# Two of the output product's four column blocks in the seven-product form, with the sums of its weights made earlier and kept in DRAM

## The chip, the core and the metric

The kernel runs on one core of a Trainium2 chip. TensorE (PE in the profile) multiplies matrices, with a weight-load side (PEld) that overlaps it; VectorE (DVE), ScalarE (ACT) and GpSimd (POOL) work element by element; SyncE (SP) issues transfers. Each engine runs its instructions in the order of its own list and waits on semaphores for the others. Transfers are issued from SP, ACT or POOL queues and carried by 16 DMA engines. SBUF is the core's working memory of 128 partitions, PSUM holds TensorE's results in eight banks of 128 x 512 fp32.

The metric is the device time of one execution in microseconds, as the median of the runs. The profile is of one execution, with times counted from the start of its span.

## The reference, cut to what matters

A decoder layer on 256 rows of 2048 channels, all in float32. The input projection gives the pieces for 16 heads of causal attention and for a short gated convolution, and the gates that merge the two:

```
h = _rmsnorm(x, pre_norm_g)
proj = jnp.einsum('bsd,de->bse', h, w_in)
...
y_mla = jnp.einsum('bse,ed->bsd', attn, w_o_mla)
...
y_conv = jnp.einsum('bse,ed->bsd', b_gate * conv * jax.nn.silu(z_conv), w_o_conv)
merged = jax.nn.sigmoid(g_mla) * y_mla + jax.nn.sigmoid(g_conv) * y_conv
out = jnp.einsum('bsd,de->bse', merged, w_out)
x = x + _rmsnorm(out, post_norm_g)
```

The change is in the last product, `merged` (256 x 2048) by `w_out` (2048 x 2048).

## The kernel before, in words

**Three matmuls for one product.** Every fp32 operand is split into a high part, rounded to the matmul's format, and a low part, the rest. A product is high x high + low x high + high x low. Weights come from DRAM in units of 128 x 2048 (1 MB); one unit holds four blocks of 128 contraction rows by 512 output columns. `load_raw` (L152) brings a unit into one of three buffers (tag raw) on SP's queue. `split_unit` (L176) splits it in two halves of 128 x 1024: ScalarE writes the high half (`whi`, L265), VectorE subtracts it from the raw weights (`wlo`, L266). There are five buffers each for high and low halves, two and a half units. `ahead` (L212) keeps loads three units and splits one unit ahead of `take` (L223), which hands a unit to the product.

**The stages.** First the latent products of the input, to about 50 us. Then 16 heads (L994 to L1113): each multiplies four units of channel weights (`channels`), and between them stand the gates' units (z), the keys', queries' and values' products, the scores, the softmax and the values of the head before. `next(form_steps)` is called three times in each of the heads 0 to 13; it runs a generator, `make_forms` (L869), one step at a time, which makes parts of sums of the normalised input on VectorE and ScalarE and stores them to DRAM from ScalarE's queue. The attention output of head group v lies in `at_f`, the channels' in `cv_f`; the blocks of groups 2 and 3 of both are first written in heads 8 and later.

From about 590 us the branch products (w_o_mla, w_o_conv, tag sq) are interleaved with the gate products g_mla and g_conv (tags sX, sY, sZ). Those gate products already use a seven-product form (Strassen's, in Winograd's arrangement): two column blocks by two halves of the contraction would take eight half products; seven products Q1, V5, V6, V7, V3, V4, Q2 of sums of input blocks (the forms) by sums of weight blocks give the same, with some additions on the results. Each is two units of 12 matmuls. Their PSUM banks are X (tag st), Z (tag cv) and Y (tag o).

Last comes the output product. The merged activations, turned so that the contraction lies on partitions, are written to DRAM in four blocks `far_m` and come back on the POOL queue into `turned_m` tiles; `split_turned` (L970) splits them into `m_b[0..3]`, for each of two row halves t one ScalarE and one VectorE instruction of 128 x 512. Blocks 2 and 3 are the last to be merged, at the end of the branch stage. Column block c needs units (c, 0..3), one for each `m_b[k]`; each plain unit is 24 matmuls (`out_products`, L1471): two row halves by four by three. The order is that of `out_order` (L145): (0,0), (0,1), (1,0), (1,1), (0,2), (1,2), (0,3), (1,3), then blocks 2 and 3. `out_block` (L1497) takes a finished PSUM bank: ScalarE squares it with a row sum, VectorE multiplies it by the gain into `og`. Block 3 runs row half by row half; `finish` and `finish_by_two` (L1527, L1533) then compute the row norm, add the residual `xr` (a 2 MB load on SP's queue, L1561) and store.

**What sets the order.** The program is traced in Python and a scheduler places each engine's instructions. An instruction that is wrapped in `keep_in_program_order` is placed behind the one traced just before it on its engine, whatever that was; one that is not wrapped may be moved ahead, as its data and the scheduler's estimate allow. All matmuls are kept. The splits of the output product's weights and of `m_b[2]` are not kept in the kernel before (`split_act`, L264, has `keep` False there); that of `m_b[3]` isn't either.

Of the kernel before, what the change touches and what calls it, by code (L numbers as in the profile page):

```python
# [82 lines left out]
def tile_layer(ctx: ExitStack, tc: tile.TileContext, xw, w0, xb, x, pos, pvec, post_g, wc, wz, wcv, wkr, wqk, wqr, wv, cwr, wsq, out):  # L83
# [92 lines left out]
    def split_unit(i):  # L176
# [22 lines left out]
        for h in range(0, w, HALF):  # L199
            n = min(HALF, w - h)  # L200
            if u_out[3, 0] <= i < u_out[3, 3]:
# [21 lines left out]
    def take(i):  # L223
        ahead(i)
        return pieces(splits.pop(i))
# [643 lines left out]
    def make_forms():  # L869
# [49 lines left out]
        while True:  # L919
            yield  # L920

    form, sums = {}, {}

# [6 lines left out]

    form_steps = make_forms()
    tap, coming, ps_by_head = None, [], {}
# [12 lines left out]

    def turned_unit(far, both, first, tag=None, queue=nc.sync):

# [3 lines left out]
        def load():  # L951
            name = f"turned_{both.name}{first}"
            if tag:
# [13 lines left out]

        return [[load if i == 0 else None, split(i), None, None] for i in range(len(far))]

# [24 lines left out]
    for h in range(H):  # L994
# [48 lines left out]
        if h < H - 2:  # L1043
            next(form_steps)
        if v and at == 0 or h == H - 1:
            next(tap)
# [21 lines left out]
        if h < H - 2:  # L1068
            next(form_steps)
        channels(h, 2)  # L1070
        if h < H - 2:
            next(form_steps)
        if h == H - 1:
            split_branch(1)
            bring_form("11")
# [48 lines left out]
    spool = right.enter_context(tc.tile_pool(name="spool", bufs=1, side="right", reuse_waits="tile"))  # L1124
    LAST = ("f5", "f6", "rb0", "rc0", "rc1", "rb1")
    last_parts = []
# [247 lines left out]
    m_b = Late("m", lambda i: spool.tile([P, 4, 2 * S], F32R, name=f"m_both{i}", tag=M_TAGS[i], bufs=1))  # L1374
    m_load = [turned_unit(far_m[a:b], m_b, a, tag, nc.gpsimd) for a, b, tag in ((0, 2, "rc0"), (2, 3, "rc1"), (3, 4, "rb1"))]

# [89 lines left out]
    assert not wanted and not fetched  # L1466

    m_load[1][0][0]()
    last_m = m_load[2][0]
# [9 lines left out]

    pss = [[bank(f"out{c}_{t}") for t in range(NT)] for c in range(2)]  # L1480
    for i, (c, kk) in enumerate(out_order[:4]):
        w = take(u_out[c, kk])
        if i == 0:
            last_m[0]()
        elif i == 2:
            m_load[1][0][1]()
        out_products(pss[c], w, kk)
    main.close()
# [7 lines left out]

    def out_block(c, t, ps):  # L1497
        cs = slice(512 * c, 512 * c + 512)
        junk = op.tile([P, 512], F32, name=f"junk{c}_{t}", tag="junk", bufs=2)
        nc.scalar.activation(junk[:, :], ps[:, :], AF.Square, accum_out=ssq[:, t, c : c + 1])  # L1500
        if c == 3 and t:
            return ps
        og_now = nc.vector.tensor_tensor(og[:, t, cs], ps[:, :], gb[:, cs], op=ALU.mult)
        if c == 3:
# [50 lines left out]

    for i, (c, kk) in enumerate(out_order[4:6]):
        w = take(u_out[c, kk])
        if i == 0:
            last_m[1]()
        out_products(pss[c], w, kk)  # L1560
    tc.keep_in_program_order(nc.sync.dma_start(out=xr[:, :, :], in_=x))  # L1561
    for c in range(3):
        if c == 2:
            pss.append([bank(f"out{c}_{t}") for t in range(NT)])
        for kk in range(4) if c == 2 else (3,):
            out_products(pss[c], take(u_out[c, kk]), kk)
        for t in range(NT):
            out_block(c, t, pss[c][t])
    nc.vector.reduce_sum(part[:, :], ssq[:, :, :3], axis=mybir.AxisListType.X)
    nc.vector.tensor_scalar(part[:, :], part[:, :], 1.0 / D, EPS, op0=ALU.mult, op1=ALU.add)  # L1570
    pss = [bank(f"out3_{t}") for t in range(NT)]
# [97 lines left out]
```

## Time and profile before

| | us |
|---|---|
| median of 3 runs (lowest, highest) | 1013.35 (1012.68, 1013.49) |
| the profiled execution's own time | 1013.55 |
| its span | 1011.8 |
| TensorE busy | 1004.2 (99%) |
| weight loads busy | 835.4 (83%) |
| VectorE busy | 811.4 (80%) |
| ScalarE busy | 586.3 (58%) |
| GpSimd busy | 170.7 (17%) |
| output product in the chain: start, length | 916.51, 87.05 |
| HBM read and written | 234.80 MB, 22.02 MB |

The granted TensorE clock is 1.00 in all the long stretches. A row of the chain of waits or of the timeline has the start, the length, the engine, what it writes and reads, and how many instructions are merged in it; in brackets stands the idle time before it and what ended that. A row of the busy time by stretch has the stretch, then for PE, PEld, DVE, ACT and POOL the busy time and the number of instructions, then the mean granted clock, the DMA engines' busy share and GB/s.

### The profile page before, as it was taken

The numbers are of one execution on the slowest core, as the hardware profiler recorded it, in microseconds if no ns is written. First come the engines' busy times: TensorE is split into PE (matmuls) and PEld (weight loads), VectorE is DVE, ScalarE is ACT, GpSimd is POOL, SyncE is SP. The second block draws the span as 40 slices with busy tenths as digits, with TensorE's granted clock in tenths as the row PEclk, the third lists the DMA queues.
The fourth block names the chain that finished last, engine by engine and source line by source line (L and its number), as shares of the span: only waits on it lengthen the run. The fifth ranks groups of instructions, "written<-read, shape, count | busy, mean of one in ns | idle before, by whom it ended". The sixth has DMA issues, their size and how long they took to land.

```text
span 1011.8 us, 12983 instructions
## 1 busy us (share of the span) xinstructions
PE 1004.2 (99%) x4552; PEld 835.4 (83%) x4552; DVE 811.4 (80%) x1111; ACT 586.3 (58%) x838; POOL 170.7 (17%) x311
## 2 busy tenths in 40 slices
PE   9999999999999999999999999999999999999997
PEld 7888888888888888888888888888888888888886
DVE  7588878868888689877797889898989779997562
ACT  7675656556556456555565465565675664674541
POOL 4620411113211223212133110000000001003000
PEclk9999999999999999999999999999999999999999
DMA  8785768568786668866689779897599989639742
GB/s 338 282 291 183 260 201 304 197 214 276 234 303 232 228 229 283 272 219 232 216 264 338 292 306 291 344 375 218 187 333 296 305 321 260 239 127 322 289 166 84
DMA packets 54369, 261.84 MB, mean 259 GB/s; under 512 B 8768, under 2 KB 13504, under 8 KB 29216
## 3 DMA queue, kind: packets, MB, share of 16 engines
q1 hardware_dynamic: 37728, 214.35, 57.7%
q0 software_dynamic: 12256, 38.13, 14.0%
q10 hardware_dynamic: 4320, 8.54, 2.4%
q8 instruction: 35, 0.57, 0.2%
q14 instruction: 30, 0.25, 0.1%
HBM read 234.80 MB, written 22.02 MB: 254 GB/s over the span
## 4 chain that ended last, share of the span: by engine, by line
PE 98%; DMA 1%; DVE 0%; ACT 0%; SPq 0%; issue 0%
PE cv L88 34%; PE sq L88 17%; PE sX L88 9%; PE z L88 9%; PE out L88 9%; PE sZ L88 4%; PE kn L88 2%; PE qn L88 2%; PE vv L88 2%; PE sY L88 2%; PE ckv L88 2%; PE qa L88 2%; PE qr L88 1%; PE o L88 1%; PE sw L88 1%; DMA raw<-xb_dram 1%
## 5 line engine op out<-in xcount | busy, mean ns | idle before, releaser
L265 ACT ACTIVATE whi<-raw 128x1024 fp32r<-128x1024 f32 (+1 forms) x302 | 306.1, 1028 | 236.7 <-PE cv L88 103.9
L266 DVE TENSOR_TENSOR wlo<-raw,whi 128x1024 fp32r<-128x1024 f32 (+1 forms) x300 | 352.7, 1188 | 101.2 <-ACT whi L265 74.6
L88 PE MATMUL cv<-whi,x_both 128*128 128x512 f32 x1024 | 319.8, 389 | 0.0
L88 PEld LDWEIGHTS cv<-whi,x_both 128*128 128x128 f32 x1024 | 192.3, 188 | 39.5
L88 PE MATMUL cv<-wlo,x_both 128*128 128x512 f32 x512 | 199.5, 390 | 0.0
L88 PEld LDWEIGHTS cv<-wlo,x_both 128*128 128x128 f32 x512 | 96.2, 188 | 19.4
L266 DVE TENSOR_TENSOR slo_V<-b,shi_V 128x1024 fp32r<-128x1024 f32 x60 | 71.5, 1218 | 15.9 <-PE sq L88 8.5
L265 ACT ACTIVATE shi_V<-b 128x1024 fp32r<-128x1024 f32 x60 | 61.5, 1053 | 39.2 <-PE sq L88 21.2
L88 PE MATMUL z<-whi,x_both 128*128 128x512 f32 x256 | 80.0, 389 | 0.0
L366 POOL DMA_DIRECT2D far<-via x64 | 35.4, 559 | 227.2 <-DVE via L358 217.2
L88 PE MATMUL sq<-whi,at_both 128*128 128x512 f32 x256 | 60.6, 389 | 0.0
L88 PE MATMUL sq<-whi,cv_both 128*128 128x512 f32 x256 | 60.6, 389 | 0.0
L88 PEld LDWEIGHTS sq<-whi,cv_both 128*128 128x128 f32 x256 | 48.0, 188 | 10.0
L88 PEld LDWEIGHTS sq<-whi,at_both 128*128 128x128 f32 x256 | 48.0, 188 | 10.0
L88 PEld LDWEIGHTS z<-whi,x_both 128*128 128x128 f32 x256 | 48.1, 188 | 9.9
L88 PE MATMUL z<-wlo,x_both 128*128 128x512 f32 x128 | 49.8, 389 | 0.0
L88 PE MATMUL out<-whi,m_both 128*128 128x512 f32 x208 | 49.4, 389 | 0.0
L88 PE MATMUL sX<-shi_V,form 128*128 128x512 f32 x192 | 47.4, 389 | 0.0
L88 PEld LDWEIGHTS out<-whi,m_both 128*128 128x128 f32 x208 | 39.0, 188 | 8.1
L88 PEld LDWEIGHTS sX<-shi_V,form 128*128 128x128 f32 x192 | 36.0, 188 | 7.5
L265 ACT ACTIVATE shi_Q<-b 128x1024 fp32r<-128x1024 f32 x28 | 28.8, 1052 | 21.5 <-PE sq L88 19.1
L1263 POOL DMA_DIRECT2D b<-wsq_dram x8 | 7.0, 869 | 193.4 <-DVE b L1272 76.8
(304 smaller groups left out, 1568.7 us busy)
## 6 DMA issues: line engine op xcount, KB each, us to landing
raw<-wcv_dram SPq DMA_DIRECT2D x64, 1024.0 KB, 6.2
raw<-wsq_dram SPq DMA_DIRECT2D x48, 1024.0 KB, 7.2
b<-wsq_dram SPq DMA_DIRECT2D x26, 1024.0 KB, 5.7
raw<-wz_dram SPq DMA_DIRECT2D x16, 1024.0 KB, 4.9
raw<-wqk_dram SPq DMA_DIRECT2D x8, 1024.0 KB, 6.8
b<-wsq_dram POOLq DMA_DIRECT2D x8, 1024.0 KB, 11.0
far_form<-form ACTq DMA_DIRECT2D x28, 256.0 KB, 3.3
form<-far_form SPq DMA_DIRECT2D x7, 1024.0 KB, 13.8
```

What stands on the lines that cost most here:

```text
L88: return tc.keep_in_program_order(nc.tensor.matmul(*a, **kw))
L265: a = nc.scalar.activation(hi, src, AF.Copy)
L266: b = nc.vector.tensor_tensor(lo, src, hi.bitcast(F32), op=ALU.subtract)
L366: tc.keep_in_program_order(queue.dma_start(out=f[i], in_=m))
L1263: tc.keep_in_program_order(nc.gpsimd.dma_start(out=dst[:, :], in_=wsq[n, c + b, k], accum_op=ALU.add))
```

## The change

Column blocks 1 and 2 of the output product are computed together by the seven products; blocks 0 and 3 stay plain, and block 3's units 0 and 1 are moved up into the middle, for both row halves. The input forms are made from the unsplit `turned_m` tiles: V7's from blocks 0 and 1 (A11 - A21) after the third plain unit; V5's, V6's and V3's from all four blocks in two parts, `m_forms(0)` ahead of plain unit (0,2) and `m_forms(1)` ahead of V5. Each part is three VectorE sums and three splits of 128 x 512.

The weight sums of V5, V7, V6 and V4 do not depend on the input, and are made in heads 1 to 7: a second generator, `make_sums`, stepped beside `make_forms`, loads four 512 KB pieces into the still unused parts of `at_f` and `cv_f` on SP's queue, adds them in four VectorE instructions of 128 x 1024 and stores four results to DRAM on ScalarE's queue, four times over. Later they are loaded as units like any other weights. There are now 22 units where there were 16. The products' matmuls are 8 x 24 + 14 x 12 = 360 where there were 384.

The splits of all output units, of `m_b[2]` and of `m_b[3]` are now kept in program order, and so are the copies of the PSUM banks that the seven products need in between (`copied`). The additions to them (`added`) and `out_block`'s instructions are not.

```diff
-    out_order = [(0, 0), (0, 1), (1, 0), (1, 1), (0, 2), (1, 2), (0, 3), (1, 3)]
-    out_order += [(c, k) for c in (2, 3) for k in range(4)]
-    u_out = {ck: add(wsq[4, ck[0], ck[1]]) for ck in out_order}
+    SUMS = ("V5", "V6", "V7", "V4")
+    far_sum = {(n, u): dram.tile([P, UNIT], F32, name=f"far_sum{n}_{u}") for n in SUMS for u in range(2)}
+    set_raw = {"Q1": (1, 0), "V3": (2, 2), "Q2": (1, 2)}
+    out_order = [(0, 0), (0, 1), (3, 0), ("Q1", 0), ("Q1", 1), (0, 2), (0, 3), ("V5", 0), ("V5", 1), ("V6", 0), ("V6", 1), (3, 1)]
+    out_order += [(n, u) for n in ("V7", "V3", "V4", "Q2") for u in range(2)] + [(3, 2), (3, 3)]
...
-            split_act(hi[:, :n], lo[:, :n], t[:, h : h + n], i in (u_head[0][1], *u_first, *u_d[0][2][:2]), i in (u_grp["r", 0], u_grp["v", 0], u_head[0][0]))
+            split_act(hi[:, :n], lo[:, :n], t[:, h : h + n], i in (u_head[0][1], *u_first, *u_d[0][2][:2]) or i >= u_out[0, 0], i in (u_grp["r", 0], u_grp["v", 0], u_head[0][0]))
...
+    def make_sums():
...
+        for _ in range(3):
+            yield
+        for i in range(4):
+            if i:
+                put(i - 1, (2, 3))
+            bring(i, (0, 1))
+            yield
+            bring(i, (2, 3))
+            yield
+            yield
+            plus(a, a, b)
+            plus(b, b, c)
+            yield
+            put(i, (0, 1))
+            plus(c, a, c)
+            plus(d, c, d)
+            yield
+        put(3, (2, 3))
...
+    def m_part(n, j, src, sign=1.0):
+        ks = slice(4 * j, 4 * j + 4)
+        hi, lo = (m_form[n][:, ks, i, :] for i in range(2))
+        keep = tc.keep_in_program_order
+        keep(nc.scalar.activation(hi, src, AF.Copy, scale=sign))
+        if sign == 1.0:
+            keep(nc.vector.tensor_tensor(lo, src, hi.bitcast(F32), op=ALU.subtract))
...
+    def m_forms(j):
+        u = m_sum(0, j, m_raw(2 + j, 1), m_raw(j, 1), ALU.subtract)
+        w = m_sum(1, j, quarters(u), m_raw(j, 0), ALU.add)
+        m_part("V5", j, u)
+        m_part("V6", j, w, -1.0)
+        w = m_sum(1, j, quarters(w), m_raw(2 + j, 0), ALU.subtract)
+        m_part("V3", j, w)
...
+    for i, (c, kk) in enumerate(out_order[:3]):
+        if i == 0:
+            last_m[0]()
+        plain_products(c, kk)
+    m_form_7()
     main.close()
...
+    def copied(name, b, tag):
+        res[name] = wide(f"o{name}", tag)
+        tc.keep_in_program_order(nc.scalar.activation(res[name][:, :], set_bank[b][:, :], AF.Copy))
+
+    def added(name, b):
+        nc.vector.tensor_tensor(res[name][:, :], res[name][:, :], set_bank[b][:, :], op=ALU.add)
+
+    set_products("Q1", 0)
+    set_products("Q1", 1)
+    copied("a", "X", "d")
+    m_load[1][0][1](True)
+    m_forms(0)
+    plain_products(0, 2)
+    last_m[1](True)
+    plain_products(0, 3)
+    m_forms(1)
+    set_products("V5", 0)
+    for t in range(NT):
+        out_block(0, t, pss[0][t])
+    set_products("V5", 1)
     tc.keep_in_program_order(nc.sync.dma_start(out=xr[:, :, :], in_=x))
...
+    set_products("V6", 0)
+    copied("c", "Z", "a")
+    set_products("V6", 1)
+    copied("b", "X", "b")
+    plain_products(3, 1)
+    for u in range(2):
+        set_products("V7", u)
+    added("c", "X")
+    out_block(2, 1, res["c"], -1.0)
+    for u in range(2):
+        set_products("V3", u)
+    added("b", "Z")
+    out_block(2, 0, res["b"], -1.0)
+    for u in range(2):
+        set_products("V4", u)
+    out_block(1, 1, set_bank["X"])
+    for u in range(2):
+        set_products("Q2", u)
+    added("a", "Y")
+    out_block(1, 0, res["a"])
...
     for t in range(NT):
-        for kk in range(4):
+        for kk in (2, 3):
             if t == 0:
                 last.append(take(u_out[3, kk]))
-            out_products(pss, last[kk], kk, (t,))
-        ps = out_block(3, t, pss[t])
+            out_products(pss[3], last[kk - 2], kk, (t,))
+        ps = out_block(3, t, pss[3][t])
         finish_by_two(t, ps) if t else finish(t)
```

More of the change, by code (lines that the diff above doesn't have):

```diff
@@ L944, in score, with turned_unit @@
         return rest if later else rest()
-    def turned_unit(far, both, first, tag=None, queue=nc.sync):
+    def turned_unit(far, both, first, tag=None, queue=nc.sync, shared=None):
         box = []
@@ L966, in split @@
             return go
-        return [[load if i == 0 else None, split(i), None, None] for i in range(len(far))]
+        return [[load if i == 0 else None, split(i), None, None, box] for i in range(len(far))]
     def split_turned(src, both, t, keep=False):
@@ L1478, in out_products @@
         ])
-    pss = [[bank(f"out{c}_{t}") for t in range(NT)] for c in range(2)]
-    for i, (c, kk) in enumerate(out_order[:4]):
-        w = take(u_out[c, kk])
+    pss = {c: [bank(f"out{c}_{t}") for t in range(NT)] for c in (0, 3)}
+    m_raw = lambda blk, t: by_rows((m_01[0] if blk < 2 else pair_23)[:, (blk % 2) * 1024 + t * 512 :][:, :512], 4)
+    m_form = {n: spool.tile([P, KH, 2, P], F32R, name=f"m_form{n}", tag=tag, bufs=1) for n, tag in (("V5", "f5"), ("V6", "f6"), ("V7", "rb0"))}
+    m_sums = spool.tile([P, 2, KH, P], F32, name="m_sums", tag="rb1", bufs=1)
@@ new lines, in m_form_7, with stationary @@
+    def m_form_7():
+        us = [m_sum(0, j, m_raw(j, 0), m_raw(j, 1), ALU.subtract) for j in range(2)]
+        for j, u in enumerate(us):
+            m_part("V7", j, u)
+    def m_forms(j):
[5 more added lines that the diff above has]
+        m_part("V3", j, w)
+    def stationary(n, k):
+        if n in m_form:
+            return m_form[n][:, k, 0, :], m_form[n][:, k, 1, :]
+        blk, t = {"Q1": (0, 0), "V4": (2, 1), "Q2": (2, 0)}[n]
+        return [m_b[blk + k // 4][:, k % 4, o + t * P : o + (t + 1) * P] for o in (0, S)]
@@ new lines, in tile_layer, with set_products @@
+    set_bank = {}
+    BANKS = {"Q1": ("X", True), "V5": ("Z", True), "V6": ("X", False), "V7": ("X", False), "V3": ("Z", False), "V4": ("X", False), "Q2": ("Y", True)}
+    def set_products(n, u):
+        w = take(u_out[n, u])
+        b, first = BANKS[n]
+        if first and u == 0:
+            tag, bufs = {"X": ("st", 1), "Z": ("cv", 2), "Y": ("o", 1)}[b]
+            set_bank[b] = bank(f"out_set{b}", tag=tag, bufs=bufs)
+        products(
+            [
+                (set_bank[b][:, :], stationary(n, k), w(k - 4 * u, 512), first and k == 0, k == KH - 1)
+                for k in range(4 * u, 4 * u + 4)
+            ],
+            **({} if first else {"skip_group_check": True}),
+        )
@@ L1554, in finish_by_two @@
         store(t, 1536, 2048, og[:, t, cs])
[L1556 to L1560, printed above, removed]
-    tc.keep_in_program_order(nc.sync.dma_start(out=xr[:, :, :], in_=x))
[L1562 to L1568, printed above, removed]
+    res = {}
```

67 lines of the change are left out of this document (56 added, 11 removed).

## The prediction, made before the change was run

> **What bounds the kernel now.** I read the page's first part, then the chain that ended last, then TensorE's waits, then busy time by stretch.
>
> ```profile
> span 1011.8 us, 12983 instructions
> PE 1004.2 (99%) x4552; PEld 835.4 (83%) x4552; DVE 811.4 (80%) x1111; ACT 586.3 (58%) x838; POOL 170.7 (17%) x311
> ```
> ```profile
> 649.96 5.44 PE sZ L88 x24
> 655.39 5.44 PE sX L88 x24
> 660.84 5.44 PE sY L88 x24
> ...
> 916.51 87.05 PE out L88 x384
> ```
> ```profile
> PE fin L88 <- ACT dg L1541: 0.9, 1, 0.9
> PE idle L88 <- PEq L1657: 0.8, 1, 0.8
> PE qa L88 <- ACT whi L265: 0.6, 2, 0.3
> ```
> ```profile
> 600.00:700.00 100.00, 100.00 (x443) 82.81 (x442) 92.50 (x77) 59.97 (x65) 7.92 (x12) 1.00 0.89 310
> 938.27:949.15 10.88, 10.88 (x50) 9.01 (x49) 5.43 (x6) 4.23 (x5) 0.00 (x0) 1.00 0.98 397
> ```
>
> TensorE runs its list almost without a hole: its waits sum to 2.3 us, none of them inside the output product, whose 384 matmuls follow each other at 87.05 / 384 = 0.2267 us, full clock. So a matmul less is 0.2267 us less, and any new hole is paid in full. VectorE is the next engine: 92.5% busy between 600 and 700 us without holding TensorE up, but 5.43 of 10.88 us in the output product.
>
> **The gain.** Blocks 1 and 2 were 8 units of 24 matmuls; seven products of two 12-matmul units are 168 instead of 192. Removed: 24 x 0.2267 = 5.44 us, all on the path. Nothing else of TensorE's goes.
>
> **The order written by hand, and its first wait.** On the old clock the stage begins at 916.51; three plain units and Q1 take 4 x 5.44, so TensorE reaches plain unit (0,2) at 938.28. That unit reads merged block 2, m_b[2].
>
> ```profile
> 1002.49 1.07 PE L88 MATMUL out<-wlo,m_both 128*128 128x512 f32 x4
> 1003.39 1.02 PE L88 MATMUL fin<-xr,ident 128*128 128x256 f32 x4
> ```
> ```profile
> 930.15 2.01 ACT L265 ACTIVATE whi<-raw 128x1024 fp32r<-128x1024 f32 x2 [3.43 <-PE out L88]
> 932.57 1.15 ACT L265 ACTIVATE m_both<-turned_m 128x512 fp32r<-128x512 f32 x2 [0.41 <-DMA turned_m<-far_m]
> 936.76 1.15 ACT L265 ACTIVATE m_both<-turned_m 128x512 fp32r<-128x512 f32 x2
> 953.83 0.58 ACT L1500 ACTIVATE junk<-out 128x512 f32<-128x512 f32 x1
> 954.30 0.19 ACT L1500 ACTIVATION_READ_ACCUMULATOR junk<-out 128x1 f32 x1
> 1003.59 0.60 ACT L1500 ACTIVATE junk<-out 128x512 f32<-128x512 f32 x1 [8.52 <-PE out L88]
> ```
> ```profile
> 911.87 0.68 DVE L1313 TENSOR_TENSOR sa<-sa,sY 128x512 f32<-128x512 f32 x1
> 932.49 2.36 DVE L266 TENSOR_TENSOR wlo<-raw,whi 128x1024 fp32r<-128x1024 f32 x2 [3.08 <-PE out L88]
> 934.77 1.28 DVE L266 TENSOR_TENSOR m_both<-turned_m,m_both 128x512 fp32r<-128x512 f32 x2
> 937.43 0.69 DVE L266 TENSOR_TENSOR m_both<-turned_m,m_both 128x512 fp32r<-128x512 f32 x1 [1.38 <-ACT m_both L265]
> 955.39 0.68 DVE L1503 TENSOR_TENSOR og<-out,gb 128x512 f32<-128x512 f32 x1
> ```
>
> In the kernel before the split of block 2 was free to run when its data came. Now it is kept in program order, and on ScalarE the instruction traced just before it is the kept copy of Q1's bank ("copied a"), which waits for Q1's last matmul. Queued behind that copy on ScalarE are both halves of block 2's split, then the forms, and TensorE waits for them. Step by step: matmul's end to ScalarE 1003.59 - 1003.39 = 0.20; the copy, like the Square from PSUM (954.30 - 953.83), 0.5 to the next start; ScalarE's half to VectorE's 937.43 - 936.76 = 0.67; VectorE's 0.69; some 0.05 to TensorE. That is 2.1 us; one matmul can go on the high half alone (0.23), so the hole is **1.9 us** (1.6 to 2.5, the upper end if the second row half is waited for too: 0.6 more).
>
> **The second wait.** Behind block 2 VectorE has, all kept: six operations of 128 x 512 for the forms, the split of the next unit, then block 3's split, which plain unit (0,3) needs. From 939.65 (938.28 + 0.2 + 0.5 + 0.67): block 2's two, 1.28; six at about 0.62, 3.7; two hops where it waits for ScalarE's half, 0.8; ScalarE's next weight half after that, 0.35; the split, 2.36 less overlap, 2.28; block 3's first, 0.69: 948.75. TensorE would be through (0,2) at 938.28 + 1.9 + 5.44 = 945.6 and can issue one matmul. Hole: **3.0 us** (2.4 to 3.6). The two holes alone return 4.9 of the 5.44.
>
> **The run of seven products.** One unit is now 12 matmuls, 2.72 us, and still costs VectorE 2.28 and ScalarE 2.0; in the kernel before that was per 5.44. After block 3 VectorE (949.4) has a split, the second forms (4.85), a split, two output multiplications (1.3), a split: 2.28 x 3 + 6.15 = 13.0, to 962.4. TensorE ends (0,3) at 954.1, does V5 in 5.44 and wants V6's second low half 2.27 later, 961.8. Late by 0.6 and some hops: **0.8** (0 to 1.6). The plain unit (3,1) behind V6 gives 2.7 us of slack back to the queues.
>
> Then three pairs end in a chain that the next unit but one is kept behind: matmul's end 0.2, addition from PSUM 0.68, Square 0.5 + 0.19, weight half 1.05, in all 2.6 against one unit's 2.72. After V7 it just fits (0.2 for the second half). From V7's end VectorE begins that unit's low halves at 2.7 and has four in a row to 7.3; V3 ends at 5.6, so its addition, traced behind them, waits, and the chain (2.4 without the matmul's end) gives V4's second unit its weights at 9.7 where 5.6 + 2.72 = 8.3 was wanted: 1.4 late; if the addition, which is not kept, slips in between two halves, 0.3: **1.0**. After Q2 the same addition stands behind the split of (3,2), whose raw buffer V4's late split frees, so that it begins only about when Q2 ends: 2.28 + 2.4 against 2.72, 2.0 late, or 0.2 if the addition slips ahead: **1.2**. Sum for the run: 0.8 + 0.2 + 1.0 + 1.2 = **3.2** (0.6 to 5.2).
>
> **Loads.** Six more units (22 for 16), a megabyte each.
>
> ```profile
> 10.00:12.00 2.00, 2.00 (x10) 1.62 (x9) 2.00 (x5) 1.50 (x4) 0.00 (x0) 1.00 1.04 433
> 18.00:20.00 2.00, 2.00 (x10) 1.69 (x9) 2.00 (x6) 2.00 (x5) 1.83 (x3) 1.00 1.05 444
> ```
> ```profile
> DMA to landing us min/median/max: 4.7/5.6/9.2
> ```
>
> A set unit every 2.72 us asks 1.049 MB / 2.72 = 386 GB/s; the kernel's start moves 433 and 444, so the wires carry it. Latency is closer: with three buffers one turn is 4.7 landing, 3.4 split (1.05 + 2.36), about 0.4 issue, 8.5 against 3 x 2.72 = 8.2. Over eight units 0.1 each is 0.8, mostly in buffers; xr's 2 MB goes ahead of one load. I take **0.3** (0 to 1.0). The Trainium skill's page "DMA: Bandwidth & Descriptors", section Bandwidth, says that some 358 GB/s of HBM bind a core's loads; by that a set unit would take an estimated 2.93 us, and the twelve units from V5 on an estimated 2.5 us more. The 433 and 444 here disagree, so it gets no part in the sum.
>
> **The sums in the heads.** 16 loads and 16 stores of 512 KB, and 16 additions of 128 x 1024.
>
> ```profile
> 249.01 1.22 DVE L884 TENSOR_TENSOR x_area<-x_area,r_x 128x1024 f32<-128x1024 f32 x1
> 262.60 2.59 DVE L266 TENSOR_TENSOR wlo<-raw,whi 128x1024 fp32r<-128x1024 f32 x2 [0.99 <-ACT whi L265]
> 266.10 0.42 DVE L434 TENSOR_TENSOR f<-o,half 128x256 f32<-128x256 f32 x1 [0.92 <-ACT half L433]
> 272.41 0.75 DVE L266 TENSOR_TENSOR kn<-f,kn 128x256 fp32r<-128x256 f32 x2
> ```
> ```profile
> 274.26 0.28 PE L88 MATMUL sc<-kn,qn_hi 128*128 128x256 f32 x1
> ```
> ```profile
> SPq L167 <- DVE wlo L266: 603.5, 126, 12.0
> far_form<-form ACTq DMA_DIRECT2D x28, 256.0 KB, 3.3
> ```
>
> 16 x 1.22 = 19.5 us of VectorE over seven heads, two at a time. SP mostly waits for buffers (603.5 us), so its loads come early, a whole head before they are used; ScalarE's stores stand one step behind their additions, as the forms' do (3.3 us to land). The tight place is head 5, the third turn, where two additions (2.4 us) fall ahead of the keys' split: kn is done at 273.16, its reader starts at 274.26, 1.1 us of slack, and VectorE idles 0.99 + 0.92 before. Cost 0 to 1.3; I take **0.2**, most of it hidden in those gaps.
>
> **The sum.** -5.44 + 1.9 + 3.0 + 3.2 + 0.3 + 0.2 = **+3.2 us**. The profiled execution took 1013.55 (span 1011.8 and 1.75 around it), the median is 1013.35: I put the change on the median, **1016.5**. The tail after the last matmul keeps its instructions.
>
> **Rivals.** A measurement of this kernel can tell about 0.2%, 2.0 us, from no change. *Even:* the two holes come (4.9) but the run stays fed, as three set products in a row did between 649.96 and 666.3 with VectorE at 92.5%: -5.44 + 4.9 + 0.6 = +0.1, 1013.4. For it: VectorE's free half in this stage. Against: there the splits were not kept behind additions.
>
> *Faster:* the forms and both merged blocks are ready in time, and the matmuls saved are saved: 1013.35 - 5.44 + 0.6 = 1008.5. It decides once all holes sum to under 3.4 us. For it: block 2's data lay in SBUF at 932.57, almost six microseconds early. Against: the copy that stands ahead of its split on ScalarE cannot start before Q1 ends, and that hole alone is 1.9. *The saving isn't there* because the products aren't fewer: 24 less are written out, so I give this nothing.
>
> *Clock:* the second hole could let TensorE's clock fall.
>
> ```profile
> 1005.29 1.13 PE L88 MATMUL fin<-og,dg 128*128 128x256 f32 x4 [0.87 <-ACT dg L1541]
> ```
> ```profile
> 1007.50:1008.00 0.50, 0.00 (x0) 0.00 (x0) 0.27 (x1) 0.00 (x0) 0.00 (x0) 0.87 1.06 406
> 1008.00:1008.50 0.50, 0.00 (x0) 0.00 (x0) 0.00 (x0) 0.00 (x0) 0.00 (x0) 0.50 1.06 397
> ```
>
> The last matmul ends at 1006.42; in the half microsecond from 1007.50 the granted clock's mean is 0.87, then 0.50, so it fell about 1.45 us after the last work (1.1 to 1.6). A hole of 3.0 is longer, one of 1.9 hardly. No row shows how long it stays down: nothing lost, or the whole unit (0,3) at half speed, 5.44. If the climb takes as long as the fall, 1.45 us at half speed lose 0.7: 1017.2. The Trainium skill's page "TensorE: Matmul & The Clock Gate", Part 1, has it that an idle window of about 3.4 us halves the clock and as long a busy one restores it, by which the loss is an estimated 1.7 us; the trace agrees on the half, but here it fell sooner, with some work still in such a window.
>
> **How the numbers follow.** Forecast, the holes and a run that is partly starved: 0.52, with its own range 1015.4 to 1019.5. Even: 0.28. Faster: 0.12. Clock, on top of the forecast's holes: 0.08. So faster 0.12, same 0.28, slower 0.60. All low ends together (1.6 + 2.4 + 0.6) give -0.8, 1012.5; all high ends (2.5 + 3.6 + 5.2 + 1.0 + 1.3) give +8.2, 1021.5, which needs every term at its worst. The range is 1011.2 to 1020.0: it leaves out the faster case and the worst sums.
>
> **What would show it.** In the new profile TensorE should wait for m_both's split twice, once right after Q1 with ScalarE's copy ahead of it, once before (0,3) some 8.6 us on with the forms' six operations ahead of it on VectorE; lengths 1.9 and 3.0. Then short waits for weight halves in V6, V4 and the last block's second unit, behind additions and Squares; 360 matmuls in the product; none or one short wait in head 5, none on loads of over 1 us. I am wrong if the product's matmuls run without a wait after Q1, if the waits sum to under 3.4 us or over 12, if the waits name loads, or if the heads stretch by over 1.3 us.

## The result, and the profile after

The changed kernel takes 1029.76 us (median of 5 runs, 1026.08 to 1030.42) against 1013.35 for the kernel before: ratio 1.0157, 95% interval 1.0145 to 1.0168. The forecast had the sign and missed the size: +16.4 where +3.2 was worked out. The profiled execution took 1028.6 us. Its page, first part:

```profile
span 1026.8 us, 13097 instructions
PE 1005.4 (98%) x4528; PEld 831.2 (81%) x4528; DVE 853.5 (83%) x1158; ACT 603.8 (59%) x861; POOL 170.3 (17%) x311
```

TensorE has the 24 matmuls less, and still the span grew by 15.0 us. What TensorE waited for (engine, line, releaser: us in total, times, longest):

```profile
PE sc L88 <- DVE kn L276: 5.9, 1, 5.9
PE out L88 <- ACT m_both L275: 2.9, 2, 1.7
PE out L88 <- DVE m_both L276: 1.3, 2, 1.0
PE out_setX L88 <- ACT whi L275: 1.1, 1, 1.1
PE out L88 <- ACT whi L275: 1.1, 1, 1.1
PE sq L88 <- ACT whi L275: 1.0, 1, 1.0
```

The longest wait is not in the product that was rewritten but in head 5, 650 us earlier. The four entries on m_both are the two forecast holes, two waits in each. Where the span went is read from the starts of groups that both kernels have. The new chain of what ended last:

```profile
267.81 1.22 DVE cv_f L951
...
280.45 1.01 PE sc L88 x3
...
302.98 21.79 PE cv L88 x96
...
926.32 16.32 PE out L88 x72
```

The same group in the chain of the kernel before, and from the two timelines the product's first matmul, before and after, and the last group (fin), after:

```profile
294.58 21.79 PE cv L88 x96
```
```profile
916.35 3.79 PE L88 MATMUL out<-whi,m_both 128*128 128x512 f32 x16
```
```profile
926.15 3.79 PE L88 MATMUL out<-whi,m_both 128*128 128x512 f32 x16
...
1018.50 1.02 PE L88 MATMUL fin<-xr,ident 128*128 128x256 f32 x4
```

The group of 302.98 stood at 294.58 before, the first matmul at 916.35, fin at 1003.39. So the heads lost 8.4 us, the branch stage 1.4 (the wait of sq on a weight half, 1.0, is most of it), the product 5.3 (92.35 for 87.04), the tail nothing. The chain points at the heads' cause: additions of the sums (L951) stand in it, ahead of the keys.

VectorE in head 5, from the timeline (start, us, engine, line, operation):

```profile
261.32 1.18 DVE L951 TENSOR_TENSOR at_f<-at_f 128x1024 f32<-128x1024 f32 x1
263.95 1.22 DVE L951 TENSOR_TENSOR at_f<-at_f,cv_f 128x1024 f32<-128x1024 f32 x1
...
267.81 1.22 DVE L951 TENSOR_TENSOR cv_f<-at_f,cv_f 128x1024 f32<-128x1024 f32 x1
...
271.24 1.18 DVE L951 TENSOR_TENSOR cv_f<-cv_f 128x1024 f32<-128x1024 f32 x1
...
279.97 0.76 DVE L276 TENSOR_TENSOR kn<-f,kn 128x256 fp32r<-128x256 f32 x2 [0.15 <-ACT kn L275]
```

All four additions of the third turn lie ahead of the keys, 4.8 us, not two; and VectorE, which in the kernel before sat idle for 0.99 and 0.92 in this stretch, runs from 253.96 to 279.97 without one gap. kn is done at 280.73 instead of 273.16. The wait is 5.9 us and the loss 8.4: TensorE's clock fell meanwhile (busy time by stretch; the third figure from the end is the granted clock):

```profile
278.00:278.50 0.50, 0.00 (x0) 0.00 (x0) 0.50 (x2) 0.00 (x0) 0.00 (x0) 0.71 0.99 393
...
285.00:285.50 0.50, 0.50 (x4) 0.41 (x3) 0.00 (x0) 0.50 (x4) 0.00 (x0) 0.96 1.01 401
```

It fell at about 278.21 and came back at 285.04. From 280.45, when TensorE had work again, 4.6 us went by at half speed: 2.3 lost. 5.9 + 2.3 and a wait of 0.3 at 143.67 make the 8.4, but for rounding.

SyncE's queue between 195 and 300 us shows a second thing that the kernel before doesn't have. Its loads for the sums (L943) wait until the stores of the turn before have landed, and the weights stand behind them. ScalarE waits for head weights in this stretch, 11.3 us in five waits, and not once in the kernel before. SyncE's waits:

```profile
SPq L943 <- DMA far_sumV<-cv_f: 11.4, 4, 4.9
SPq L943 <- DMA far_sumV<-at_f: 8.5, 3, 5.0
```
```profile
far_sumV<-cv_f ACTq DMA_DIRECT2D x4, 512.0 KB, 8.9
far_form<-form ACTq DMA_DIRECT2D x6, 256.0 KB, 6.0
```

The last two rows (the DMA issues of the same stretch; the last number is the median time to landing) show why SyncE's wait is long: the stores take up to 8.9 us to land, and the forms' own stores, 3.3 before, now 6.0.

In the product, TensorE's timeline:

```profile
949.28 0.50 PE L88 MATMUL out<-whi,m_both 128*128 128x512 f32 x1 [1.21 <-ACT m_both L275]
950.01 3.72 PE L88 MATMUL out<-whi,m_both 128*128 128x512 f32 x15 [0.22 <-DVE m_both L276]
...
957.19 0.51 PE L88 MATMUL out<-whi,m_both 128*128 128x512 f32 x1 [1.66 <-ACT m_both L275]
958.73 3.71 PE L88 MATMUL out<-whi,m_both 128*128 128x512 f32 x15 [1.03 <-DVE m_both L276]
...
976.46 3.96 PE L88 MATMUL out<-whi,m_both 128*128 128x512 f32 x16 [1.07 <-ACT whi L275]
...
997.70 2.14 PE L88 MATMUL out_setX<-whi,m_both 128*128 128x512 f32 x8 [1.10 <-ACT whi L275]
```

The two units behind the two holes take 7.46 us (947.91 to 955.37) and 8.72 (to 964.09) instead of 5.44 each: 2.0 and 3.3 more. V5 to Q2 with (3,1) take 42.24 for 38.08, the last block 12.17 for 10.88.

### The profile page after: what moved, and what is told of

Its sections match the earlier page's. It is cut to its first block, busy times and chain, and to the rows that moved or that the text cites. A ratio compares the mean times of both kernels' runs of the same rounds, so it can differ in the third digit from the quotient of the medians.

```text
span 1026.8 us, 13097 instructions
## 1 busy us (share of the span) xinstructions
PE 1005.4 (98%) x4528; PEld 831.2 (81%) x4528; DVE 853.5 (83%) x1158; ACT 603.8 (59%) x861; POOL 170.3 (17%) x311
## 4 chain that ended last, share of the span: by engine, by line
PE 85%; DVE 7%; DMA 4%; issue 2%; ACT 1%; DVEq 0%; ACTq 0%
PE cv L88 29%; PE sq L88 16%; PE sX L88 8%; PE z L88 8%; PE sZ L88 4%; PE out L88 3%; DVE wlo L276 3%; DMA raw<-wsq_dram 2%; PE qa L88 2%; PE sY L88 2%; PE ckv L88 2%; PE vv L88 2%; PE kn L88 2%; PE qn L88 2%; PE out_setX L88 1%
## 5 line engine op out<-in xcount | busy, mean ns | idle before, releaser
L275 ACT ACTIVATE whi<-raw 128x1024 fp32r<-128x1024 f32 (+1 forms) x318 | 321.4, 1028 | 232.3 <-PE cv L88 89.9
L276 DVE TENSOR_TENSOR wlo<-raw,whi 128x1024 fp32r<-128x1024 f32 (+1 forms) x316 | 371.1, 1189 | 91.2 <-ACT whi L275 80.6
L276 DVE TENSOR_TENSOR slo_Q<-b,shi_Q 128x1024 fp32r<-128x1024 f32 x28 | 33.5, 1220 | 6.2 <-PE sq L88 5.1
L1329 DVE TENSOR_TENSOR b<-b,b 128x2048 f32<-128x2048 f32 x16 | 36.5, 2284 | 0.0
```

Source lines behind the costliest of these rows:

```text
L275: a = nc.scalar.activation(hi, src, AF.Copy)
L276: b = nc.vector.tensor_tensor(lo, src, hi.bitcast(F32), op=ALU.subtract)
L1329: nc.vector.tensor_tensor(t[:, :], t[:, :], raw[plus][:, :], op=ALU.add)
```

## The experiments

Each kernel was timed beside the kernel before on the same chip, whose medians were 1012.98 to 1013.39; each result gives the ratio with its interval. I had two questions: which part of make_sums costs the heads 8.4 us, and whether the product's loss is the order of its queues.

**e1, the product alone.** The sums are not made; V5, V6, V7 and V4 read weights that nothing was added to, so only the time means something.

```diff
-            u_out[n, k] = add(far_sum[n, k][:, :])
+            u_out[n, k] = add(wsq[4, 1 if n in ("V5", "V4") else 2, k + (0 if n in ("V5", "V7") else 2)])
...
-            next(sum_steps)
```

> The seven products with all their input forms, but no weight sums: the units of V5, V6, V7 and V4 are loaded from the unsummed weights, so the output is another one, with the same loads and matmuls. If the heads' loss (TensorE reaches the output product 9.8 us late) comes from making the sums, the product starts here at 916.5 as in the kernel before, and the median is about 1013.35 + 5.3 = 1018.6: the stage's 92.2 us against 86.9. If the loss is the scheduler's new order of the whole program, the product starts late here too and the time stays near 1029.

1018.8 us, 1.0053 (1.0038 to 1.0068), no wait in the heads. The product's own loss is 5.7 us; the rest of the 16.4 belongs to make_sums. This run also showed what the changed kernel's profile did not. The 15 matmuls behind the second hole took 3.71 us there, and here:

```profile
948.61 5.11 PE L88 MATMUL out<-whi,m_both 128*128 128x512 f32 x15 [1.03 <-DVE m_both L276]
```
```profile
948.00:949.00 1.00, 0.40 (x1) 0.40 (x2) 1.00 (x2) 1.00 (x2) 0.00 (x0) 0.63 0.09 33
...
951.00:952.00 1.00, 1.00 (x5) 0.80 (x4) 1.00 (x2) 0.00 (x0) 0.00 (x0) 0.66 0.97 410
```

The clock was at half from 948.26 to 951.67 and cost 1.4 us. So the rival "Clock" is real, though it strikes in one execution and not in another.

**e2, the sums alone**: the kernel before with make_sums, its results read by nobody.

```diff
-    form_steps = make_forms()
+    form_steps, sum_steps = make_forms(), make_sums()
...
+            next(sum_steps)
```

> The kernel before with the weight sums made in heads 1 to 7 and never read; the output product is the plain one. If all of the late start is the making of the sums, 1013.35 + 9.8 = 1023, with a wait of TensorE on the keys' split in head 5 of about 6 us and a fallen clock behind it; if the output product's part is the larger, it stays under 1017.

1021.23, 1.0079 (1.0064 to 1.0094), with the wait of sc on kn at 5.4 us. The heads' loss needs nothing of the new product.

**e3, the transfers alone** (e2 without its additions) and **e4, the additions alone** (e2 with the first turn's loads and no stores):

```diff
-            plus(a, a, b)
-            plus(b, b, c)
...
-            plus(c, a, c)
-            plus(d, c, d)
```
```diff
-            if i:
-                put(i - 1, (2, 3))
-            bring(i, (0, 1))
+            if i == 0:
+                bring(i, (0, 1))
...
-            put(i, (0, 1))
...
-        put(3, (2, 3))
```

> As the sums alone, but without the sixteen additions: what is loaded is stored as it is. If SP's queue is the cause (weight loads behind sum loads that wait for stores), most of the loss stays: 1018 to 1023. If the additions on VectorE are the cause, 1013 to 1014. If it takes both, 1013 to 1015 here and in the additions alone.

> As the sums alone, but with the four loads of the first round only and no stores: sixteen additions in the same places. If the additions are the cause, 1018 to 1023, with a wait on the keys' split in head 5; if SP's queue is the cause, 1013 to 1014; if it takes both, 1013 to 1016.

e3: 1024.66, 1.0110 (1.0085 to 1.0135). e4: 1020.38, 1.0068 (1.0051 to 1.0085). Either half alone costs about as much as both, the transfers even more: neither "one of them" nor "both add" holds. They lose in different places:

```profile
PE o L88 <- DVE pt L268: 5.0, 1, 5.0
PE sc L88 <- DVE kn L268: 2.0, 1, 2.0
PE cv L88 <- ACT cv_w L810: 1.8, 1, 1.8
```
```profile
SPq L935 <- DMA far_sumV<-at_f: 24.2, 6, 7.9
SPq L935 <- DMA far_sumV<-cv_f: 17.4, 5, 5.2
```
```profile
PE sc L88 <- DVE kn L268: 4.5, 1, 4.5
```

The first two fences are e3's: three waits at different places, and SyncE held for 41.6 us between 100 and 420 by loads that wait for stores. The clock adds to them: in e3's trace it is at half in three stretches of 3.41 us (from 167.66, 280.30 and 304.20), some 5 us. The third is e4's: one wait, head 5, as in the changed kernel. Two theories then: the additions cost through their place ahead of head 5's keys, the transfers through SyncE's queue. Each got an experiment that moves what it names.

**e6, the additions of the third turn behind head 5's keys** (e4 with two steps more before them; two steps are left out of the fourth turn, so that it keeps its place):

```diff
...
+            if i == 2:
+                yield
+                yield
             plus(a, a, b)
```

> The additions alone (first loads only, no stores, results unread, as in e4), the third round's four additions placed behind head 5's keys instead of ahead of them. Theory (the loss is the place in head 5, where the keys had 1.1 us to spare): the wait sc <- kn of 4.5 us and the fallen clock go; 1013.5 to 1015.5. Rival (39 us of additions reach VectorE's queue somewhere else with the same result, since the other instructions are ordered anew around them): another wait of 3 us or more in heads 1 to 8, 1018 to 1022.

1013.58, 1.0003 (0.9994 to 1.0012): the same 16 additions, and nothing is lost. TensorE's waits are the kernel before's two of 0.9 and 0.8 and one of 0.3.

**e7, the loads of the sums on GpSimd's queue** (e3 with one word changed):

```diff
-                keep(nc.sync.dma_start(out=area[n], in_=wsq[4, blk, k][:, h * w : (h + 1) * w]))
+                keep(nc.gpsimd.dma_start(out=area[n], in_=wsq[4, blk, k][:, h * w : (h + 1) * w]))
```

> The transfers alone (no additions, results unread, as in e3), the loads of the sums on GpSimd's queue instead of SyncE's, so that no weight load stands behind a load that waits for a store. Theory (the weights are late because SyncE's queue is held): most of e3's 11 us go, 1013.5 to 1017. Rival (the DMA engines are full: 16 MB more in 180 us, weights of 11 to 13 us to land whichever queue asks): 1020 to 1026, and raw loads still land 11 us after their issue.

1015.07, 1.0020 (1.0007 to 1.0032), where e3 had 1024.66, and TensorE's longest wait is 1.3 us. The bytes are the same, so the volume alone is not it: with the choice of the queue 9.6 us go. By which step is not shown. Late weights are not enough: between 100 and 420 us ScalarE waits for them in e3 (first of the next two) no more than in e7 (second).

```profile
ACT whi L267 <- DMA raw<-wcv_dram: 14.9, 6, 4.8
```
```profile
ACT whi L267 <- DMA raw<-wcv_dram: 21.8, 8, 6.0
```

The head weights land as late, too: 7.4 us in the median in e3 and 7.3 in e7, and the slowest weight load took 12.9 and 14.0. In e3 TensorE's 5.0 us stand at the end of a chain behind the slowest: ScalarE's half of pt came behind the half of a weight that was issued at 289.24, when VectorE had freed its buffer, and took 12.86 to land. The Trainium skill's page "DMA: Bandwidth & Descriptors", section Rules for kernel authors, has it that spreading transfers over the queues brings no bandwidth and saves only issue time; the equal landing times agree, and yet 9.6 us are saved here, with SyncE no longer held by loads that wait for stores.

A rival stands beside the held queue. The one word changed VectorE's order too: in e7, as in the kernel before, a split of pt (119.26) stands ahead of rs (120.14), in e3 rs (117.86) comes first, and from there on the two lists differ. What of the 9.6 us is the queue and what the order that the scheduler made around it was not separated.

**e8, the additions on GpSimd** (e4 with another engine):

```diff
-            keep(nc.vector.tensor_tensor(o, x, y, op=ALU.add))
+            keep(nc.gpsimd.tensor_tensor(o, x, y, op=ALU.add))
```

> The additions alone (first loads only, no stores, results unread, as in e4), on GpSimd instead of VectorE. Theory (VectorE's work ahead of head 5's keys is the price): the wait sc <- kn goes, 1013.3 to 1015. Rival (GpSimd's additions take several us each and hold the transfers that it issues for the turned tiles and the taps, or slow VectorE beside them): waits of 3 us and more on tiles that GpSimd brings, 1017 or more.

1036.77, 1.0240 (1.0217 to 1.0262), the worst of all: the rival, and more.

```profile
L943 POOL TENSOR_TENSOR at_f<-at_f,cv_f 128x1024 f32<-128x1024 f32 x4 | 11.8, 2952 | 0.3
```
```profile
L268 DVE TENSOR_TENSOR kn<-f,kn x16: 415/418/2630, 84.7 to 561.5; 128x256 fp32r<-128x256 f32 x16
```

The additions of the group shown take 2.95 us on average there for VectorE's 1.22 (all sixteen 2.4 to 3.4), and VectorE's own operations stretch beside it: the split of kn (shortest, median, longest in ns) took 2630 once instead of 418. The Trainium skill's page "SBUF — State Buffer", section SBUF: two separate sides, says that GpSimd and a VectorE operation with two SBUF inputs exclude each other for a whole instruction; the 2630 agrees: that split began at 282.47, beside an addition that ran to 284.82, and ended at 285.10. The profiled execution is the fastest of the four, 1032.89 us, 19.5 above the kernel before. TensorE's waits that the kernel before doesn't have make 13.4 of it, and three stretches of 3.41 us at half clock (from 169.27, 288.73 and 346.76), in which it was busy for 9.63, another 4.8.

**e5, the product with its two splits first** (on e1; m_both3's split ahead of forms(0)):

```diff
     set_products("Q1", 0)
+    m_load[1][0][1](True)
     set_products("Q1", 1)
     copied("a", "X", "d")
-    m_load[1][0][1](True)
-    m_forms(0)
+    last_m[1](True)
     plain_products(0, 2)
-    last_m[1](True)
+    m_forms(0)
     plain_products(0, 3)
```

> The product alone (its sums not made: V5, V6, V7 and V4 read unsummed weights, as in e1), with the split of m_both2 placed before Q1's second unit and that of m_both3 right behind the copy of Q1's bank, ahead of forms(0), which moves behind (0,2). Theory (both holes are the order of ScalarE's and VectorE's queues): the waits of 1.87 and 3.13 us go, 1018.8 falls by about 5 to 1013.8, and the waits of PE out on m_both fall below 0.5 us together. Rival (the holes are the landing of m's pieces or of the weights, or the forms just become late for V5 in their place): 1016.5 to 1019, with a wait of out_setZ on m_form in the list.

1017.72, 1.0044 (1.0029 to 1.0059): a miss, in the rival's range. Both waits on m_both are gone, but one of 5.11 us stands in their place, at V5's second unit, and behind it the clock is at half from 954.30 to 961.13, so that the unit's 12 matmuls take 5.03 us for 2.72. ScalarE shows the wait's cause:

```profile
950.87 0.63 ACT L1550 ACTIVATE m_formV<-m_sums 128x512 fp32r<-128x512 f32 x1 [0.94 <-DVE m_sums L1558]
952.66 0.63 ACT L1550 ACTIVATE m_formV<-m_sums 128x512 fp32r<-128x512 f32 x1 [1.17 <-DVE m_sums L1558]
954.78 0.63 ACT L1550 ACTIVATE m_formV<-m_sums 128x512 fp32r<-128x512 f32 x1 [1.48 <-DVE m_sums L1558]
955.31 5.78 ACT L275 ACTIVATE whi<-raw 128x1024 fp32r<-128x1024 f32 x6
```

The weight halves for V5's second unit stand behind forms(1), a chain that goes back and forth between VectorE and ScalarE three times. V5 needs only the first of the three forms.

**e9, the forms apart**: e5 with V5's sums and parts placed behind (0,2), V6's behind (0,3), V3's behind (3,1), and block 0's outputs behind V5 (the last two not shown).

```diff
+    us = [m_sum(0, j, m_raw(2 + j, 1), m_raw(j, 1), ALU.subtract) for j in range(2)]
+    ws = [m_sum(1, j, quarters(us[j]), m_raw(j, 0), ALU.add) for j in range(2)]
+    for j in range(2):
+        m_part("V5", j, us[j])
     plain_products(0, 3)
+    for j in range(2):
+        m_part("V6", j, ws[j], -1.0)
...
```

> The product alone (V5, V6, V7 and V4 read unsummed weights, as in e1 and e5), with e5's splits and with the forms taken apart: V5's two sums and parts during (0,2), V6's during (0,3), V3's only behind (3,1); the block 0 outputs behind V5. Theory (e5's wait of 5.11 us was V5's second unit behind the whole of forms(1), which V5 needs a third of): that wait goes, no other of over 1.5 us comes, and 24 matmuls less begin to show: 1010.5 to 1013. Rival (VectorE simply has more work than TensorE gives it time for from Q1 to V6): the wait comes back at another unit, 1015 to 1018.

1015.78, 1.0027 (1.0016 to 1.0038): a miss of the theory's range; the time is in the rival's, the cause is not VectorE's work. V5 starts as if there had been no hole; 2.48 us are lost at (3,1), where ScalarE waits for a weight load that was issued 3.1 us behind xr's 2 MB (952.12 and 949.06) and took 8.6 to land, and 0.5, 1.1 and 1.1 in the three pairs behind it.

**e13, e9 with xr's load ahead of (0,2), V3's parts a unit earlier and the closing additions a unit later**:

```diff
     copied("a", "X", "d")
+    tc.keep_in_program_order(nc.sync.dma_start(out=xr[:, :, :], in_=x))
...
+    set_products("V3", 0)
     added("c", "X")
     out_block(2, 1, res["c"], -1.0)
-    for u in range(2):
-        set_products("V3", u)
+    set_products("V3", 1)
+    set_products("V4", 0)
     added("b", "Z")
...
```

> The product alone (unsummed weights, as in e1, e5 and e9), e9's order with three moves more: the 2 MB load of xr ahead of (0,2) instead of inside the run of seven products, V3's parts one unit earlier, and the closing additions and outputs of V7, V3 and V4 one unit later, behind the next weight split. Theory (what e9 kept was the weights behind xr's load, 2.48 us at (3,1), and the split of the next unit behind closings that wait for VectorE, 0.5 and 1.1 and 1.1 us): 1010.5 to 1012.5. Rival (the run is bound by VectorE's or the DMA engines' work, 7 units of 2.72 us each needing 2.35 of splits and 2.45 of transfer): 1014 to 1016.

1012.39, 0.9995 (0.9986 to 1.0004). The kernel with 168 matmuls for the two blocks now takes as long as the one with 192, not less. From 1018.8 to 1012.4 only the order was changed: the loss of e1 was order. Which of e13's three moves counts was not separated.

**e10, e11, e12 and e14: the heads again, with one remedy or both.** e12 is e2 with e6's place for the third turn, loads still on SyncE. e11 is the whole change with e6's place and e7's queue, e10 the same with e9's product. e14 is e12 with the loads on ScalarE's queue, one step behind the stores that free their place; its diff, cut, is against e2.

```diff
-                keep(nc.sync.dma_start(out=area[n], in_=wsq[4, blk, k][:, h * w : (h + 1) * w]))
+                keep(nc.scalar.dma_start(out=area[n], in_=wsq[4, blk, k][:, h * w : (h + 1) * w]))
...
+            if i == 2:
+                yield
+                yield
             plus(a, a, b)
```

> The sums alone, unread (as in e2), the third round's additions behind head 5's keys, but the loads still on SyncE's queue. Theory of two separate prices (the transfers alone cost 11 us in e3): 1017 to 1024, with waits on weights or on what stands behind them. Rival (head 5's place was all, and what e3 lost belongs to its own order of VectorE's work): 1013 to 1015.5.

> The whole change with its product as it is, only the heads mended: the third round's additions behind head 5's keys and the loads of the sums on GpSimd's queue. Theory (heads 0 to 2 us, product +5.4 as in e1): 1018.5 to 1021. Rival (the heads' loss has a third part that neither touches): 1024 to 1030.

> The whole change with the order of e9, the additions of the third round behind head 5's keys, as in e6, and the loads of the sums on GpSimd's queue, as in e7. If the prices add as the theory has it (product with e9's order, heads at the 0 to 2 us that e6 and e7 left): 1010.5 to 1015, no wait of sc on kn. Rival (transfers and additions together still make head 5 late, or the branch stage finds less spare): over 1018.

> The sums alone, unread (as in e2 and e12), the third round's additions behind head 5's keys and the loads on ScalarE's queue, a call behind the stores that free their place. Theory (e12 lost 6 us because SyncE's queue was held, e11 2 to 3 us because GpSimd's was): 1013.3 to 1015.5. Rival (16 MB of transfers in 200 us cost this much on any queue, by later landings): 1017 to 1020.

e12: 1019.4, 1.0060 (1.0045 to 1.0074): with the additions out of their bad place and the loads still on SyncE, 6.3 us are left, in other waits than e3's (2.3 on kn, 2.1 and 1.1 elsewhere). e11: 1023.15, 1.0099 (1.0086 to 1.0112); e10: 1021.2, 1.0086 (1.0066 to 1.0106). e11 misses its range by 2.2 us, e10 by 6.2, with executions from 1018.80 to 1027.15: 2.0 and 2.4 us of the wait on kn are left. In e10 one of the four additions still falls between the keys' two halves, and VectorE waits 2.63 us for a turned tile that GpSimd brings back late:

```profile
274.46 0.42 DVE L755 TENSOR_TENSOR at_f<-f,at_f 128x256 f32<-128x256 f32 x1 [2.63 <-DMA at_f<-far]
...
279.69 1.22 DVE L951 TENSOR_TENSOR at_f<-at_f 128x1024 f32<-128x1024 f32 x1
280.83 0.42 DVE L276 TENSOR_TENSOR kn<-f,kn 128x256 fp32r<-128x256 f32 x1
```

e14: 1014.87, 1.0021 (1.0012 to 1.0030). On ScalarE's queue, behind the stores themselves, the same loads cost less: 4.4 us of e12's 6.3 are gone. The head weights land no sooner (7.6 us in the median, 7.5 in e12), and VectorE's order differs here too.

**e15, the whole change with e13's product and e14's sums**:

> The whole change with the product of e13 and the sums of e14. If the parts add: 1013.1 plus what e13 and e14 differ from it, 1010.5 to 1015. Rival (the stages are not apart, the sums shift what the branch stage or the product finds): over 1017.

1014.13, 1.0015 (1.0004 to 1.0026) against 1.0157 for the change as made. The parts add: e13's -0.6 and e14's +1.9 make +1.3, and +1.15 was measured. The two largest of TensorE's waits in it that the kernel before doesn't have:

```profile
PE out_setX L88 <- DVE wlo L276: 0.8, 2, 0.5
...
PE cv L88 <- ACT cv_f L814: 0.8, 1, 0.8
```

It doesn't beat the kernel before, and none of these kernels does.

## Why the prediction was right or wrong

**The gain** was as forecast: 24 matmuls, 5.44 us.

**The two holes** were right in place, cause and size: 1.9 and 3.0 were forecast, waits of 1.21, a matmul and 0.22 and of 1.66, one matmul and 1.03 were measured: from the unit before to the second matmul, less one matmul, 950.01 - 947.91 - 0.23 = 1.87 and 958.73 - 955.37 - 0.23 = 3.13. e5 shows the cause, for both vanish with the order. What the prediction did not see is that the forms behind the splits had no time to spare either.

**The run of seven products** was sized too small: 3.2 and 0.3 for loads were forecast, 4.2 and 1.3 in the last block were lost, 5.5 in all. V4's second unit came as forecast (1.0; 1.10 and its slower start). The loads term failed: (3,1) alone waited 1.07 us behind a load that ScalarE waited 2.96 for. The changed kernel's chain:

```profile
967.78 1.23 DVE wlo L276
969.03 6.24 DMA raw<-wsq_dram
```

The load went out only when VectorE's split had freed its buffer, 7 us behind xr's (962.0), and took 6.24 us. In e9 xr's 2 MB just ahead made the load at this place late. The sentence "xr's 2 MB goes ahead of one load" had that without a price of its own; the late split it did not have.

**The step that failed** is "The sums in the heads": 0.2 where 8.4 were lost. That is 8.2 of the 13.2 us between forecast and median; 2.3 are the product's, 1.4 the branch stage's, for which there was no term, and the profiled execution took 1.2 less than the median. Three of the step's reasons were wrong. "SP mostly waits for buffers, so its loads come early": true of weight loads, but the new loads wait for stores and hold SyncE (41.6 us in e3); with them on another queue 9.6 us are gone (e7). "ScalarE's stores 3.3 us to land": 8.9 with this traffic. "Two additions (2.4 us) fall ahead of the keys' split": four did, 4.8 us, as the order of VectorE's queue around them came out anew, and the gaps that were to hide them were gone (in e4, without one store, VectorE is busy for 11.00 of the 11 us from 258 to 269). The place itself, head 5 with its 1.1 us of slack, had been named; e6, where the place alone is changed, shows that it was the additions' whole price. And the end "1.3" took only the additions against the slack, with nothing for the clock, which made 8.4 of 5.9. Two of the prediction's own signs of being wrong came: the heads stretched by over 1.3 us, and a wait in the product led back to a load.

**The rivals.** Even and Faster are out for the change as made; e13 is Even, by another order. Clock was given 0.08 for the product: it didn't strike in the changed kernel's profile, struck in e1's (1.4 us; 0.7 forecast), in e11's at the same hole and in e5's behind the hole of 5.11, and in the changed kernel it struck in head 5, where no rival had it. The changed kernel's other four executions, of which there is no trace, had a mean granted clock of 0.993 or 0.994 for 0.996 in the profiled one, so it may have struck there once more. The two prices in the heads do not add (e3 and e4 alone 11.6 and 7.3, together 8.2 in e2): in e2 the wait on the keys, 5.4, is the only one left of e3's three. Why e3's other two are not in it was not tried; VectorE's order differs between the two kernels.

**What stays open.** e15's product still takes 85.84 us where 168 + 192 matmuls at 0.2267 are 81.6: 3.6 of it in V5 to Q2, in pieces under 1 us behind VectorE's and ScalarE's halves. Whether any order feeds units of 2.72 us was not settled. The 1.0 us wait in the branch stage was seen in the changed kernel's profile; the branch stages of e1, e10, e11 and e15 run without it, and its cause wasn't tried; the chain has a weight load there that took 13.58 us to land. And how the queue of the sums' loads reaches TensorE was not read from the traces, nor parted from VectorE's order that changed with it: moving the loads off SyncE took 9.6 us away (e3 to e7) and 4.4 (e12 to e14), while the weights landed no sooner.

## What to carry to other kernels

A side job that runs under a busy TensorE is not priced by its busy time but by the tightest reader behind it on each queue it enters: find that reader's slack (1.1 us here) and count all that can land ahead of it, not what program order shows. A transfer that waits for another transfer is better kept off the queue of the loads that the bound engine needs: it cost 9.6 and 4.4 us there, though by which step stays open. And a saving in matmuls counts only when the engines that feed the shorter units have that much time: here the order alone was worth 6.3 us (e1 to e13), more than the whole saving of 5.44.

## What the runs showed of the hardware

The granted clock fell and came back at a fixed beat, not some time after the last matmul as the prediction had it from the tail (1.45 us). From fall to return: 3.41 us in e1 (948.26 to 951.67 in the trace's clock record), in e11 and three times in e3; 6.83, twice 3.41, in the changed kernel (278.21 to 285.04) and in e5. The stretches between fit the same beat: the changed kernel's first one at full clock, 5.14 to 278.21, is 273.07 us long, 80 times 3.413. The falls came 3.7 us (changed kernel) and 4.8 (e3's last) after the last matmul's end, and in e1 across a hole with one matmul in it. The Trainium skill's page "TensorE: Matmul & The Clock Gate", Part 1, speaks of a free-running window of 3413 ns; the traces agree.

What decides, as far as the traces go, is TensorE's work in the beat that ends. In e1 the beat before the fall held 1.06 us of it (first row). In the changed kernel the same hole lies across two beats, counted on from 285.04, with 1.75 and 2.38 us (the other two rows), and the clock stayed up:

```profile
944.85:948.26 3.41, 1.06 (x4) 0.32 (x2) 3.15 (x4) 3.41 (x5) 0.00 (x0) 1.00 0.00 0
```
```profile
954.05:957.46 3.41, 1.75 (x8) 1.09 (x6) 2.45 (x4) 3.37 (x5) 0.00 (x0) 1.00 0.00 0
957.46:960.87 3.41, 2.38 (x10) 1.80 (x10) 3.41 (x5) 2.10 (x3) 0.00 (x0) 1.00 0.45 147
```

In all the traces the falls came behind beats with 0 to 1.60 us of work, and the emptiest beat that passed without a fall had 1.51 (e10), the next 1.65 (e9): the limit lies near half a beat. The tail's 1.45 us were no delay but the end of such a beat (1004.46 to 1007.87, 1.13 us of work). So a hole of 3 us costs 3 us or 4.4, by where it falls in the beat.

A megabyte's landing depends on what else is under way: between 195 and 300 us the head weights' median was 6.5 us in the kernel before and 7.5 in the changed one, where a group of the stores of 512 KB took 8.9 in the median.
